# A fifth landing tile for weight pieces, a later split of the probabilities, and two overlapped output quarters in a two-layer decoder trunk

## The chip, the cores and the metric

The kernel runs on one core of one Trainium2 chip. The metric is the device time of one execution in microseconds (us). The kernel before took 2178.07 us, the median of three runs (2176.98 to 2179.72).

## What is computed

The reference runs two decoder layers on 256 tokens of width 2048, all in float32. Layer 0 mixes with a gated spatial unit and a linear recurrence (mixer A and B), layer 1 with 16 heads of attention that has a forget gate (mixer C). Each mixer is followed by a gated MLP with a short convolution.

```python
for l in range(DEPTH):                       # DEPTH = 2
    h = rms_norm(x, mix_norm[l])
    if l % 2 == 0:
        h = mixer_ab(h, ab_w_in[j], ...)     # 2048 -> 6144 columns, then w_out 2048 x 2048
    else:
        h = mixer_c(h, c_w_in[j], ...)       # 2048 -> 4 * 2048 + 16 columns, then w_out
    x = x + h
    h = rms_norm(x, ffn_norm[l])
    x = x + conv_ffn(h, ffn_w_up[l], ...)    # 2048 -> 2 * 5632, conv of width 3, 5632 -> 2048

# mixer C, for each block of 128 queries and each head:
s = q @ k.T * scale + c[query] - c[key]      # c: running sum of the log of the forget gate
p = softmax(where(causal, s, -inf))
o = p @ v
return (concat(o) * sigmoid(g)) @ w_out
```

## The kernel before, in words

**Weights.** Every weight is read once, in pieces of 128 x 1024 numbers (512 KB). A piece is good for 12 matmuls of 512 columns: two rows of 128 inputs (k and k + 1), two halves T of the tokens, and three products each, because every float32 operand is split in a high part and a rest that together carry the precision (high x high, high x low, low x high). One piece is called a step here. `weights` makes a piece: `three` takes a landing tile `w` and two tiles `wh` and `wl`, SyncE (SP) issues the load of `w`, ScalarE (ACT) copies `w` to `wh` (L178), VectorE (DVE) subtracts to get `wl` (L179), and TensorE (PE) then reads `wh` and `wl`. The tile `w` comes free when its `wl` is made. The main pool has four tiles `w` and three of `wh` and `wl` (`wpool, pool, nw, ns = wp, wp, 4, 3`). In the MLPs two of every five pieces, after the twelfth, use tiles of a second pool, and in mixer C every fourth piece has its `wh` and `wl` in one.

**Order.** Loads of `w`, copies to `wh` and subtractions to `wl` each keep the order of the pieces. Everything else is a Python generator that `tick` moves on by one `yield` a step, so that a `yield` is a delay by one piece. `held` keeps an instruction behind the newest `wh` or `wl`. What a queue holds next to the pieces, and where, follows from that and from the order in which the framework lays the instructions out; the engines then run their queues in order.

**Turning.** Matmuls give tokens on partitions; many steps need features there. `blocks` turns 32 x 32 blocks on DVE, `moves` then sends 16 small transfers of 32 KB (L360), eight on SP's queue and eight on GpSimd's (POOL), from `tmp` to a tile that is named `turn`, `dst`, `o` or `zt`.

**Attention (mixer C).** Four groups of four heads; for each group three projections of eight steps (q, k, v), by `project_tok`. `turn_rows` normalises and turns q and k. `attend` works on two heads: it copies and splits their q and k (`k`, `kk`, `qq`, L1012 to L1016), multiplies them, takes the softmax, turns the probabilities by 16 transfers from POOL (`pt`, L1058), waits `LAG + 2` = 8 yields, splits `pt` in `ph` (ACT, L1067) and `pl` (DVE, L1068), and multiplies with v; ACT copies the result to `o` (L1082). After the groups come four steps-of-eight projections for the gate (`w_cg`); `gate` multiplies the gate, turned, with `o` (DVE, L1160) and splits the products into `yc` (ACT L392, DVE L394), four of them for each quarter.

**Output of attention.** `w_co` is multiplied in four quarters q of 512 output columns, each over all 16 `yc` (k = 0, 2, ... 14), by `project_four`; `product(k)` gives `yc` number k. Then `add_four` turns the result and adds it to `x`. The output of mixer A and B, in layer 0, has another order: the last two pieces of its quarter 0 come after four pieces of quarter 1 (the function `stretch` of that mixer).

**Small tiles.** The constants `cst` hold four blocks of 128 columns, the last of them, K_REV, a reversed identity. `ra` and `rb` serve one reversal of row scales in `mirror`; `rs` is a tile of 64 columns for each of the four groups, of which eight columns are used.

Of the kernel before, what the change touches and what calls it, by code (L numbers as in the profile page):

```python
# [8 lines left out]
F32 = mybir.dt.float32  # L9
F32R = mybir.dt.float32r  # L10
U16 = mybir.dt.uint16
AF = mybir.ActivationFunctionType
ALU = mybir.AluOpType
AX = mybir.AxisListType

P = 128
S = 256
D = 2048
KT = D // P
NH = 8  # L20
CH = 16
# [3 lines left out]
BLK = 32  # L25
LAG = 6
# [7 lines left out]
LANE = 64  # L34
# [11 lines left out]
K_ID, K_TRI, K_CM, K_REV = 0, 128, 256, 384  # L46
NK = K_REV + P
# [7 lines left out]
def tile_trunk(ctx: ExitStack, tc: tile.TileContext, x, pp_d, cst_d, mlev_d, msk_d,  # L55
               w_v, w_f, w_g, w_i, w_q, w_u, w_abo, w_cf, w_cqkv, w_cg, w_co, w_up, w_dn, spw_d, spb_d, out):
    nc = tc.nc
    V, SC, PE = nc.vector, nc.scalar, nc.tensor

    cp = ctx.enter_context(tc.tile_pool(name="cp", bufs=1))  # L60
    wp = ctx.enter_context(tc.tile_pool(name="wp", bufs=4))
    apool = ctx.enter_context(tc.tile_pool(name="ap", bufs=KT))
    tp = ctx.enter_context(tc.tile_pool(name="tp", bufs=2))
# [4 lines left out]
    def nm(base):  # L68
        count[0] += 1
        return f"{base}_{count[0]}"  # L70

    xT = []
    xload = []
    for c0, n in ((0, 1), (1, 1), (2, 2), (4, 2), (6, 2), (8, 4), (12, 4)):
        t = cp.tile([P, n, S], F32, tag=f"x{c0}", name=f"x{c0}")
# [1 line left out]
        xT += [t[:, i] for i in range(n)]  # L77
    part = {c0 + i: (t, i, c0 + n - 1) for t, c0, n in xload for i in range(n)}
    pp = cp.tile([P, -(-NPP // LANE) * LANE], F32, tag="pp", name="pp")
    cst = cp.tile([P, NK], F32, tag="cst", name="cst")  # L80
    ones = cp.tile([P, P], F32, tag="ones", name="ones")
    one1 = cp.tile([P, LANE], F32, tag="one1", name="one1")[:, 0:1]

# [40 lines left out]
    flight, queue = [], []  # L124
# [38 lines left out]

    def three(n):
        deep["turn"] += 1
        wpool, pool, nw, ns = wp, wp, 4, 3
        if deep["pool"] is not None:
            if deep["more"] == 2 and deep["turn"] > 12 and deep["turn"] % 5 in (1, 3):
                wpool, pool, nw, ns = deep["pool"], deep["pool"], 2, 2
            elif deep["more"] == 1 and deep["turn"] % 4 == 3:  # L170
                pool, ns = deep["pool"], 1
        w = wpool.tile([P, n], F32, tag="w", name=nm("w"), bufs=nw)
        wh = pool.tile([P, n], F32R, tag="wh", name=nm("wh"), bufs=ns)
        wl = pool.tile([P, n], F32R, tag="wl", name=nm("wl"), bufs=ns)
        return w, wh, wl
# [150 lines left out]
    def project_four(w4, acts, n, k0=0, ks=None, ps=None, more=False):  # L326

        begun = ps is not None
        ps = ps or [pm.tile([P, 512], F32, tag="pm", name=nm("pm")) for _ in range(2)]
        ks = ks or range(0, n, 2)  # L330
        for k in ks:
            tick()
            lo = (k0 + k) * P
            wh, wl = weights(w4[:, :, lo:lo + 2 * P].rearrange("m p c -> p m c"), 1024, 4)
            for T in range(2):
                for i in range(2):
                    a = acts(k + i) if callable(acts) else acts[k + i]
                    ah, al = a[:, T * P:(T + 1) * P], a[:, S + T * P:S + (T + 1) * P]
                    h, l = (by_rows(t, i) for t in (wh, wl))
                    PE.matmul(to_rows(ps[T]), ah, h, start=not begun and k + i == ks[0], stop=False)  # L340
                    PE.matmul(to_rows(ps[T]), ah, l, start=False, stop=False)  # L341
                    deep["mm"] = deep["last"] = PE.matmul(to_rows(ps[T]), al, h, start=False,  # L342
                                                          stop=not more and k + i == ks[-1] + 1)
        return ps
# [39 lines left out]
    def held(r, last="wh"):  # L384

        tc.add_manual_dep(r.ins, deep[last].ins.name, order, reason="not before")
# [69 lines left out]
            rsq(Rt, p2[:, 0:4].rearrange("p (t two) -> p t two", two=2)[:, :, 0], D)  # L456
            self.Rt = Rt

    def add_x(m, ps):
        t = tp.tile([P, S], F32, tag="ev", name=nm("ev"), bufs=3)  # L460
        SC.activation(t, ps[:, S:2 * S], AF.Copy)
        V.tensor_tensor(xT[m], xT[m], ps[:, 0:S], ALU.add)
        V.tensor_tensor(xT[m], xT[m], t, ALU.add)

    def add_four(q, ps, z, tmp, dst, nxt, halves=1, queues=(nc.sync, nc.gpsimd)):
        for T in range(2):
            SC.activation(cols4(z[:, T]), of_rows(ps[T]), AF.Copy)
# [23 lines left out]
    def mixer_ab(norm):  # L491
        es = ExitStack()
        hp = es.enter_context(tc.tile_pool(name="hp", bufs=1))
# [19 lines left out]
        for g, ps in enumerate(project_first(w_v, norm, lambda: queue.append(finish()))):  # L513
            v = hp.tile([P, 2, 512], F32, tag="tok", name=nm("gv"), bufs=2)
# [10 lines left out]
        def fetch_late(*args, behind="wh"):  # L525
            r = SC.dma_start(*args)
            tc.add_manual_dep(r.ins, deep[behind].ins.name, order, reason="queue order")

        fetch_late(cst, cst_d, behind="hold")
        fetch_late(pp[:, C_FFN:C_CW], pp_d[:, C_FFN:C_CW], behind="hold")  # L530
        def wide(n):
            return hp.tile([P, 1024], F32, tag="QK", name=nm(n), bufs=2)
# [77 lines left out]


        Rr = hp.tile([P, LANE], F32, tag="Rr", name="Rr")[:, 0:2]
        ra, rb = (hp.tile([P, LANE], F32, tag=n, name=n)[:, 0:BLK] for n in ("ra", "rb"))

        def mirror():
            yield
            held(V.tensor_copy(ra, Rt[:, 1:2].to_broadcast([P, BLK])), "wl")
            V.tensor_copy(Rr[:, 0:1], Rt[:, 0:1])
            V.transpose(rb, ra)
            V.transpose(ra, view(rb, BLK - 1, (-1, BLK)))  # L620
            for a in range(4):
                V.tensor_copy(Rr[BLK * (3 - a):BLK * (4 - a), 1:2], ra[BLK * a:BLK * (a + 1), 0:1])
# [41 lines left out]
        for j in range(2):  # L664
            ps = project_four(w_f[4 * j:4 * j + 4], A, KT)
# [3 lines left out]
            t = hp.tile([P, 1024], F32, tag="o", name=nm("turn"), bufs=2)  # L669
# [5 lines left out]
        itoks, left, os_ = [], [NH], []  # L675
# [154 lines left out]
        for h in range(NH):  # L830
# [6 lines left out]
            ps = project(w_q[h], A)  # L837
            for T in range(2):
                q = kq[h][:, 2 - T]
                SC.activation(back(q) if T else q, view(ps, T, (2, P)), AF.Copy, scale=omlb[:, h:h + 1])  # L840
            queue.append(hgrn(h))
        for j in range(2):
            ps = project_four(w_g[4 * j:4 * j + 4], A, KT)
# [16 lines left out]
        for j in range(2):  # L860
            ps = project_four(w_u[4 * j:4 * j + 4], A, KT)
# [3 lines left out]
            t = hp.tile([P, 1024], F32, tag="tok", name=nm("turn"), bufs=2)  # L865
# [15 lines left out]
        ahead = None  # L881
        for q in range(4):
            if q == 0:

                ps = stretch(0, (0, 2, 4, 6, 8, 10), more=True)
                ahead = stretch(1, (0, 2, 4, 6), more=True)
                stretch(0, (12, 14), ps=ps)
            elif q == 1:
                ps = stretch(1, (8, 10, 12, 14), ps=ahead)
            else:  # L890
                ps = stretch(q, range(0, KT, 2))
# [11 lines left out]
    def mixer_c(norm):  # L903
        es = ExitStack()
        hp = es.enter_context(tc.tile_pool(name="cpool", bufs=1))
# [86 lines left out]
            V.tensor_copy(ct, ps[:, 0:S].rearrange("p (t c) -> p t c", t=2)[..., 0:CH])  # L992

        left, soft = [CH], [CH]
        os_, rss = [], []

        turn = [0]

        def attend(hs, q, k, v, o, rs, mark):

            while len(mark) < 2 or steps[0] < max(turn[0], mark[1] + LAG + 2):
                yield
# [45 lines left out]
            for i, sms in enumerate(sums):  # L1048
                t = V.transpose(tmp.rearrange("p (b m i) -> p b m i", b=4, m=6)[:, :, 3 * i:3 * i + 3],
                                sc[:, 3 * i:3 * i + 3].rearrange("p m (b j) -> p b m j", b=4))  # L1050
# [3 lines left out]
            n = 6 * BLK  # L1054
            pt = hp.tile([P, 6, P], F32, tag="pt", name=nm("pt"), bufs=2)
            for a in range(4):
# [3 lines left out]
                                        .rearrange("p (m r) -> p m r", m=6))  # L1060
                if a == 1:
                    yield
            for _ in range(LAG + 2):
                yield
            pair = [hp.tile([P, 2, S], F32R, tag=n, name=nm(n), bufs=1) for n in ("ph", "pl")]
            near = pt.rearrange("p (i m) q -> p i (m q)", i=2)[:, :, 0:S]
# [43 lines left out]
        for g in range(CH // 4):  # L1110
            qkv, mark = [], []
            ss = hp.tile([P, 2, 2, LANE // 4], F32, tag="ss", name=nm("ss"), bufs=2)[..., 0:4]
            for j in range(3):
                if g == 0 and j == 2:
                    cd = []
                    queue.append(sums(*forget()))
                if g and j == 2:
                    spread(g)
                ps = early[j] if g == 0 and j < 2 else project_tok(w_cqkv[j * (CH // 4) + g], norm)
                if j == 2:  # L1120
                    vs = [hp.tile([P, 512], F32R, tag=n, name=nm(n), bufs=2) for n in ("vh", "vl")]
                    v1 = hp.tile([P, 512], F32, tag="v", name=nm("v"), bufs=2)
                    SC.activation(cols2(vs[0]), of_two(ps[0]), AF.Copy, scale=Rt[:, 0:1])
                    SC.activation(cols2(v1), of_two(ps[1]), AF.Copy, scale=Rt[:, 1:2])
                    V.scalar_tensor_tensor(cols2(vs[1]), of_two(ps[0]), Rt[:, 0:1], cols2(vs[0]).bitcast(F32),
                                           ALU.mult, ALU.subtract)
                    qkv.append((vs, v1))
                    break
                t = piece("turn", 4)
                start(turn_rows(ps, ss, j, heads(t), mark))  # L1130
                qkv.append(heads(t))
            if g == 0:
                columns(cd[1])
            os_.append(heads(piece("o", CH // 4)))
            rss.append(hp.tile([P, LANE], F32, tag="rs", name=nm("rs"), bufs=CH // 4)[:, 0:8]
                       .rearrange("p (t h) -> p t h", t=2))
            queue.extend(attend((h, h + 1), *qkv, os_[g], rss[g], mark) for h in range(4 * g, 4 * g + 4, 2))

        room, places = [], [("big", 4, 1)] + 2 * [("vh", 1, 2), ("vl", 1, 2)] + 4 * [("o", 2, CH // 4)]
        depth[0] = 3  # L1140
# [30 lines left out]
        for q in range(CH // 4):  # L1171
            ps = project_four(w_cg[4 * q:4 * q + 4], A, KT)
# [4 lines left out]
        def product(k):  # L1177
            while yB[k] is None:
                tick()
            return yB[k]  # L1180

        nxt = Norm(C_FFN + KT, turn=True)
        depth[0] = 2
        for q in range(4):
            ps = project_four(w_co[4 * q:4 * q + 4], product, KT)
            add_four(q, ps, piece("z", 2), flat(piece("tmp", 2)), heads(piece("turn", 4)), nxt)
        deep["pool"] = None
        es.close()
# [232 lines left out]
```

## Time and profile before

| | |
|---|---|
| median of 3 runs | 2178.07 us |
| the profiled execution | 2179.36 us |
| its span | 2177.6 us |
| PE busy | 2167.3 us (100%) |
| DVE busy | 1599.6 us (73%) |
| ACT busy | 1313.4 us (60%) |
| POOL busy | 472.0 us (22%) |
| granted clock of PE | 1.00 in every stage |

The profiled execution's time lies 1.8 us above its span, and 1.3 us above the median. Busy time of PE counts each matmul from its start to a modelled end, 0.38 us for 512 columns, though the next one starts after 0.216 us; so a hole of PE shows in the profile as idle time only beyond about 0.16 us, and is read better from the starts of the matmuls. Layer 0's mixer lies at 0 to 392 us of the span, its MLP at 392 to 1063 us, mixer C at 1063 to 1515 us, and its MLP after that.

### The profile page before, as it was taken

How to read it: one execution, taken by the hardware profiler on the slowest of the kernel's cores; microseconds unless marked ns; L12 is line 12 of the kernel's file. 1: busy time of each engine (PE TensorE's matmuls, PEld its weight loads, DVE VectorE, ACT ScalarE, POOL GpSimd, SP SyncE). 2: the span in 40 equal slices, each digit the busy share in tenths (PEclk: the TensorE clock that was granted, in tenths of full speed). 3: DMA queues.
4: the chain of work that ended last, by engine and by line, in shares of the span. 5: the costliest groups of instructions: out<-in, count | busy, mean ns of one | idle time of the engine just before them, and what ended most of it. 6: DMA issues, size and time to landing. Idle time of an engine off the chain costs nothing.

```text
span 2177.6 us, 32602 instructions
## 1 busy us (share of the span) xinstructions
PE 2167.3 (100%) x10874; PEld 1900.8 (87%) x10874; DVE 1599.6 (73%) x2286; ACT 1313.4 (60%) x1951; POOL 472.0 (22%) x865
## 2 busy tenths in 40 slices
PE   9999999999999999999999999999999999999999
PEld 8988888888888888888888888888888888888888
DVE  7788768777567757776987786877776577667766
ACT  7678766666556545654565566766666466456642
POOL 0252222212012002111133444212211012011202
PEclk9999999999999999999999999999999999999999
DMA  8655687877676766776777767777777677766866
GB/s 300 205 164 175 200 243 225 249 229 236 210 226 209 237 210 210 229 241 206 234 227 229 219 216 215 223 238 235 231 227 240 196 230 219 228 213 204 255 211 189
DMA packets 492617, 483.62 MB, mean 222 GB/s; under 512 B 115136, under 2 KB 460240, under 8 KB 492320
## 3 DMA queue, kind: packets, MB, share of 16 engines
q1 hardware_dynamic: 465888, 453.27, 66.6%
q0 software_dynamic: 24832, 25.92, 5.1%
q10 hardware_dynamic: 1728, 2.35, 0.3%
q8 instruction: 85, 1.39, 0.3%
q14 instruction: 84, 0.69, 0.1%
HBM read 435.24 MB, written 2.11 MB: 201 GB/s over the span
## 4 chain that ended last, share of the span: by engine, by line
PE 90%; DVE 3%; DMA 2%; ACT 2%; issue 1%; SPq 1%; POOL 0%; ACTq 0%; DVEq 0%; POOLq 0%
PE pm L341 25%; PE pm L342 25%; PE pm L340 25%; PE pm L322 3%; PE pm L321 3%; PE pm L323 3%; PE pm L297 1%; DVE wl L179 1%; PE pm L229 1%; SPq L360 1%; ACT wh L178 1%; PE pm L253 1%; DMA pt<-ptmp 1%; DMA w<-in_w_f 0%; DVE kq L734 0%
## 5 line engine op out<-in xcount | busy, mean ns | idle before, releaser
L179 DVE TENSOR_TENSOR wl<-w,wh 128x1024 fp32r<-128x1024 f32 (+1 forms) x820 | 990.5, 1218 | 452.4 <-ACT wh L178 440.5
L178 ACT ACTIVATE wh<-w 128x1024 fp32r<-128x1024 f32 (+1 forms) x820 | 855.4, 1049 | 611.7 <-PE pm L342 437.4
L341 PE MATMUL pm<-wl,a 128*128 128x512 f32 x1728 | 655.6, 379 | 0.9 <-DVE wl L179 0.8
L340 PE MATMUL pm<-wh,a 128*128 128x512 f32 x1728 | 655.9, 380 | 0.0
L342 PE MATMUL pm<-wh,a 128*128 128x512 f32 x1728 | 654.9, 379 | 0.0
L360 POOL DMA_DIRECT2D zt<-tmp x413 | 224.3, 551 | 1133.8 <-DVE tmp L353 1021.7
L341 PEld LDWEIGHTS pm<-wl,a 128*128 128x128 f32 x1728 | 326.6, 189 | 49.0 <-DVE wl L179 3.1
L340 PEld LDWEIGHTS pm<-wh,a 128*128 128x128 f32 x1728 | 326.5, 189 | 46.2
L342 PEld LDWEIGHTS pm<-wh,a 128*128 128x128 f32 x1728 | 326.6, 189 | 46.1
L340 PE MATMUL pm<-wh,hid 128*128 128x512 f32 x688 | 260.8, 379 | 0.0
L341 PE MATMUL pm<-wl,hid 128*128 128x512 f32 x688 | 260.8, 379 | 0.0
L342 PE MATMUL pm<-wh,hid 128*128 128x512 f32 x688 | 260.8, 379 | 0.0
L322 PE MATMUL pm<-wl,a 128*128 128x512 f32 x416 | 158.2, 380 | 2.5 <-DVE wl L179 2.4
L321 PE MATMUL pm<-wh,a 128*128 128x512 f32 x416 | 158.6, 381 | 0.0
L323 PE MATMUL pm<-wh,a 128*128 128x512 f32 x416 | 157.8, 379 | 0.0
L342 PEld LDWEIGHTS pm<-wh,hid 128*128 128x128 f32 x688 | 130.0, 189 | 18.5
L340 PEld LDWEIGHTS pm<-wh,hid 128*128 128x128 f32 x688 | 130.0, 189 | 18.5
L341 PEld LDWEIGHTS pm<-wl,hid 128*128 128x128 f32 x688 | 130.0, 189 | 18.4
L360 POOL DMA_DIRECT2D turn<-tmp x160 | 87.2, 553 | 244.0 <-DVE tmp L353 156.1
L1227 ACT ACTIVATE conv<-zt,pp 128x256 f32<-128x256 f32 x176 | 95.8, 589 | 65.8 <-DMA zt<-tmp 54.0
L1228 DVE SCALAR_TENSOR_TENSOR conv<-zt,pp,conv 128x255 f32<-128x255 f32 x176 | 80.1, 480 | 49.6 <-ACT conv L1227 33.4
L353 DVE STREAM_TRANSPOSE tmp<-z 128x512 f32<-128x512 f32 x120 | 98.3, 856 | 7.2 <-ACT z L1213 5.1
(252 smaller groups left out, 2246.3 us busy)
## 6 DMA issues: line engine op xcount, KB each, us to landing
w<-in_w_up SPq DMA_DIRECT2D x352, 512.0 KB, 4.9
w<-in_w_dn SPq DMA_DIRECT2D x176, 512.0 KB, 4.9
w<-in_w_cqkv SPq DMA_DIRECT2D x96, 512.0 KB, 4.7
w<-in_w_abo SPq DMA_DIRECT2D x32, 512.0 KB, 4.8
w<-in_w_cg SPq DMA_DIRECT2D x32, 512.0 KB, 4.6
w<-in_w_co SPq DMA_DIRECT2D x32, 512.0 KB, 4.7
zt<-tmp SPq DMA_DIRECT2D x414, 32.0 KB, 2.6
zt<-tmp POOLq DMA_DIRECT2D x413, 32.0 KB, 2.5
```

Of the source, the lines that this page charges most:

```text
L178: r = deep["wh"] = SC.activation(wh, w, AF.Copy)
L179: deep["wl"] = V.tensor_tensor(wl, w, wh.bitcast(F32), ALU.subtract)
L321: PE.matmul(to_two(ps[T]), ah, h, start=k + i == 0, stop=False)
L322: PE.matmul(to_two(ps[T]), ah, l, start=False, stop=False)
L323: deep["last"] = PE.matmul(to_two(ps[T]), al, h, start=False, stop=k + i == KT - 1)
L340: PE.matmul(to_rows(ps[T]), ah, h, start=not begun and k + i == ks[0], stop=False)
L341: PE.matmul(to_rows(ps[T]), ah, l, start=False, stop=False)
L342: deep["mm"] = deep["last"] = PE.matmul(to_rows(ps[T]), al, h, start=False, stop=not more and k + i == ks[-1] + 1)
L353: V.transpose(tmp.rearrange("p (b m i t) -> p b m i t", b=4, m=4, t=2)[:, :, :, :, T], src(T).rearrange("p (m b j) -> p b m j", m=4, b=4))
L360: queues[(a + b) % len(queues)].dma_start(dst[BLK * b:BLK * (b + 1), :, a * n:(a + 1) * n], tmp[BLK * a:BLK * (a + 1), b * 4 * n:(b + 1) * ...
L1227: held(SC.activation(c, z, AF.Identity, bias=pp[:, cb:cb + 1], scale=w(2)))
L1228: V.scalar_tensor_tensor(c[:, 1:], z[:, :S - 1], w(1), c[:, 1:], ALU.mult, ALU.add)
```

## The change

Three edits and some that make room for them.

1. The main pool's landing tiles `w` go from four to five. The room comes from `cst`, which loses the block K_REV (nothing reads it), from `ra` and `rb`, which become two parts of a tile `junk` that exists already, and from the four tiles `rs`, which become parts of one.
2. `attend` waits `LAG + more` yields before it splits the probabilities: 11 in place of 8 for the first three groups, 8 as before for the last.
3. The last two pieces (k = 12 and 14) of quarter 0 of attention's output come after the first two pieces (k = 0 and 2) of quarter 1. Four accumulators are then open at once.

A function `add_x` that nothing called goes as well.

```diff
-    cst = cp.tile([P, NK], F32, tag="cst", name="cst")
+    cst = cp.tile([P, K_REV], F32, tag="cst", name="cst")
...
-        wpool, pool, nw, ns = wp, wp, 4, 3
+        wpool, pool, nw, ns = wp, wp, 5, 3
...
-        fetch_late(cst, cst_d, behind="hold")
+        fetch_late(cst, cst_d[:, 0:K_REV], behind="hold")
...
-        ra, rb = (hp.tile([P, LANE], F32, tag=n, name=n)[:, 0:BLK] for n in ("ra", "rb"))
...
+            r = hp.tile([P, 512], F32, tag="junk", name=nm("junk"), bufs=1)
+            ra, rb = (r[:, i * BLK:(i + 1) * BLK] for i in range(2))
...
+        rsum = hp.tile([P, LANE], F32, tag="rs", name="rs")
...
-        def attend(hs, q, k, v, o, rs, mark):
+        def attend(hs, q, k, v, o, rs, mark, more):
...
-            for _ in range(LAG + 2):
+            for _ in range(LAG + more):
                 yield
...
-            queue.extend(attend((h, h + 1), *qkv, os_[g], rss[g], mark) for h in range(4 * g, 4 * g + 4, 2))
+            rss.append(rsum[:, 8 * g:8 * g + 8].rearrange("p (t h) -> p t h", t=2))
+            queue.extend(attend((h, h + 1), *qkv, os_[g], rss[g], mark, 5 if g < CH // 4 - 1 else 2) for h in range(4 * g, 4 * g + 4, 2))
...
+        def stretch(q, ks, **kw):
+            return project_four(w_co[4 * q:4 * q + 4], product, KT, ks=ks, **kw)
+
         nxt = Norm(C_FFN + KT, turn=True)
         depth[0] = 2
+        ahead = None
         for q in range(4):
-            ps = project_four(w_co[4 * q:4 * q + 4], product, KT)
+            if q == 0:
+                ps = stretch(0, range(0, 12, 2), more=True)
+                ahead = stretch(1, (0, 2), more=True)
+                stretch(0, (12, 14), ps=ps)
+            elif q == 1:
+                ps = stretch(1, range(4, KT, 2), ps=ahead)
+            else:
+                ps = stretch(q, range(0, KT, 2))
```

**SP's queue at the end of the last group of attention.** The rows are the loads of pieces for v (`in_w_cqkv`) and for the gate (`in_w_cg`), and the eight transfers that turn the last group's k. Before:

```order
L191 DMA w_12953<-in_w_cqkv 128x1024
L191 DMA w_12971<-in_w_cqkv 128x1024
L191 DMA w_12989<-in_w_cqkv 128x1024
L191 DMA w_13017<-in_w_cg 128x4x256
L360 DMA turn_12795<-tmp_12797 32x4x64 x8
L191 DMA w_13035<-in_w_cg 128x4x256
L191 DMA w_13069<-in_w_cg 128x4x256
```

And after:

```order
L191 DMA w_12952<-in_w_cqkv 128x1024
L191 DMA w_12974<-in_w_cqkv 128x1024
L191 DMA w_13013<-in_w_cg 128x4x256
L191 DMA w_13031<-in_w_cg 128x4x256
L360 DMA turn_12788<-tmp_12790 32x4x64 x8
L191 DMA w_13065<-in_w_cg 128x4x256
L191 DMA w_13110<-in_w_cg 128x4x256
```

One more load stands ahead of the turning transfers: two pieces of the gate in place of one.

**ACT's queue at the same place.** The rows are copies of pieces (`wh`), of the next two heads' k and q (`k`, `kk`, `qq`), the copies of v's accumulators (`vh`, `v`), and, after, the results of a pair of heads of the group before (`o`). Before:

```order
L1012 ACTIVATE k_2302_13061<-turn_12795,gq 128x128
L1013 ACTIVATE kk_13062<-turn_12795,gq 128x256
L1014 ACTIVATE qq_13063<-turn_12561 128x128
L178 ACTIVATE wh_13070<-w_13069 128x1024
L1123 ACTIVATE vh_13007<-pm_12801,Rt_10562 128x512
L1124 ACTIVATE v_13009<-pm_12802,Rt_10562 128x512
L178 ACTIVATE wh_13115<-w_13114 128x1024
L178 ACTIVATE wh_13133<-w_13132 128x1024
```

And after:

```order
L1008 ACTIVATE k_2299_13057<-turn_12788,gq 128x128
L1009 ACTIVATE kk_13058<-turn_12788,gq 128x256
L1010 ACTIVATE qq_13059<-turn_12558 128x128
L178 ACTIVATE wh_13066<-w_13065 128x1024
L1119 ACTIVATE vh_12992<-pm_12794,Rt_10561 128x512
L1120 ACTIVATE v_12994<-pm_12795,Rt_10561 128x512
L178 ACTIVATE wh_13111<-w_13110 128x1024
L1078 ACTIVATE o_12319<-px_13001 128x2x128
L1078 ACTIVATE o_12319<-px_13002 128x2x128
L178 ACTIVATE wh_13129<-w_13128 128x1024
```

The two copies to `o`, which stood three copies of pieces earlier, now follow the copies of v. The same is found at the ends of the two groups before.

**ACT's queue where the last quarter's products are made.** The rows are copies of `w_co` pieces (`wh`) and the four splits to `yc` number 12 to 15. Before, the four `wh` ahead of the first `yc` are those of quarter 0 with k = 8, 10, 12 and 14, and the next is quarter 1's first:

```order
L178 ACTIVATE wh_13996<-w_13995 128x1024
L178 ACTIVATE wh_14016<-w_14015 128x1024
L178 ACTIVATE wh_14037<-w_14036 128x1024
L178 ACTIVATE wh_14057<-w_14056 128x1024
L392 ACTIVATE yc_13992<-turn_13894 128x256 x2
L178 ACTIVATE wh_14100<-w_14099 128x1024
L392 ACTIVATE yc_14033<-turn_13894 128x256 x2
```

After, they are quarter 0's k = 8 and 10 and quarter 1's k = 0 and 2, and the next two are quarter 0's k = 12 and 14:

```order
L178 ACTIVATE wh_13992<-w_13991 128x1024
L178 ACTIVATE wh_14012<-w_14011 128x1024
L178 ACTIVATE wh_14035<-w_14034 128x1024
L178 ACTIVATE wh_14055<-w_14054 128x1024
L392 ACTIVATE yc_13988<-turn_13890 128x256
L178 ACTIVATE wh_14073<-w_14072 128x1024
L392 ACTIVATE yc_13988<-turn_13890 128x256
L392 ACTIVATE yc_14031<-turn_13890 128x256 x2
L178 ACTIVATE wh_14091<-w_14090 128x1024
```

The splits keep their place among the copies; what moved is which pieces lie ahead of them.

More of the change, by code (lines that the diff above doesn't have):

```diff
@@ L457, in finish_tok @@
             self.Rt = Rt
[L459 to L463, printed above, removed]
     def add_four(q, ps, z, tmp, dst, nxt, halves=1, queues=(nc.sync, nc.gpsimd)):
@@ L1134, in mixer_c @@
             os_.append(heads(piece("o", CH // 4)))
-            rss.append(hp.tile([P, LANE], F32, tag="rs", name=nm("rs"), bufs=CH // 4)[:, 0:8]
-                       .rearrange("p (t h) -> p t h", t=2))
-            queue.extend(attend((h, h + 1), *qkv, os_[g], rss[g], mark) for h in range(4 * g, 4 * g + 4, 2))
+            rss.append(rsum[:, 8 * g:8 * g + 8].rearrange("p (t h) -> p t h", t=2))
+            queue.extend(attend((h, h + 1), *qkv, os_[g], rss[g], mark, 5 if g < CH // 4 - 1 else 2) for h in range(4 * g, 4 * g + 4, 2))
         room, places = [], [("big", 4, 1)] + 2 * [("vh", 1, 2), ("vl", 1, 2)] + 4 * [("o", 2, CH // 4)]
```

## The prediction

> **What bounds the kernel now.** I read the page first, then the busy time by stage, the table of waits with PE's rows alone, and then the timeline around each wait of PE. The page:
>
> ```profile
> span 2177.6 us, 32602 instructions
> PE 2167.3 (100%) x10874; PEld 1900.8 (87%) x10874; DVE 1599.6 (73%) x2286; ACT 1313.4 (60%) x1951; POOL 472.0 (22%) x865
> ```
>
> PE is the bound. The stages (length, then PE's busy time and its matmuls in brackets, then the other engines) show where it has holes; the last column is what the DMA engines moved in GB/s:
>
> ```profile
> 100.00:192.00 92.00, 89.31 (x936) 81.40 (x938) 74.80 (x142) 71.31 (x199) 46.69 (x84) 1.00 0.58 174
> ...
> 392.00:1063.00 671.00, 671.00 (x3111) 587.39 (x3109) 480.47 (x644) 389.48 (x518) 112.98 (x208) 1.00 0.73 222
> ...
> 1515.00:2155.00 640.00, 640.00 (x2967) 560.41 (x2966) 451.30 (x592) 369.65 (x480) 104.41 (x193) 1.00 0.73 223
> ```
>
> In the two MLPs PE has no hole at all: 671.00 us for 3111 matmuls is 0.216 us from start to start, which no edit here changes, since the same matmuls run. So only a hole outside the MLPs can be gained. PE's waits are few:
>
> ```profile
> PE pm L322 <- DVE wl L179: 2.4, 3, 1.0
> PE pm L341 <- DVE wl L179: 1.3, 3, 0.5
> ...
> PE pm L340 <- ACT yc L392: 0.7, 1, 0.7
> ```
>
> A matmul's modelled end lies 0.16 us behind the next start, so each hole is larger than its entry. I size each by PE's starts: the time between two starts less 0.216 us for every matmul between them.
>
> **Edit 3, the overlapped quarters.** The three kinds of rows below are PE's, DVE's and ACT's timelines at the end of quarter 0 of attention's output.
>
> ```profile
> 1419.09 0.38 PE L342 MATMUL pm<-wh,yc 128*128 128x512 f32 x1
> 1420.17 0.48 PE L340 MATMUL pm<-wh,yc 128*128 128x512 f32 x1 [0.71 <-ACT yc L392]
> ...
> 1424.34 0.38 PE L340 MATMUL pm<-wh,yc 128*128 128x512 f32 x1
> ```
>
> ```profile
> 1419.00 1.43 DVE L1160 TENSOR_TENSOR turn<-turn,o 128x256 f32<-128x256 f32 x4 [2.36 <-DMA turn<-tmp]
> ```
>
> ```profile
> 1419.45 1.32 ACT L392 ACTIVATE yc<-turn 128x256 fp32r<-128x256 f32 x2 [4.08 <-DVE turn L1160]
> ```
>
> PE needs `yc` number 12 right after its row at 1419.09. The split starts at 1419.45, since the last turning transfer ended DVE's wait only at 1419.00. The row at 1424.34 is sixteen matmuls behind that at 1419.09: 5.25 - 16 x 0.216 = 1.79 us are lost. After the change 24 matmuls of quarter 1 stand there first, 24 x 0.216 = 5.2 us, for which `yc` 0 to 3 have long been made. Their pieces have their `wh` ahead of the first split in ACT's queue, as the order shows. `yc` number 12 is then wanted at 1424.5 and is there by 1421; its own piece's `wh` follows the first split (1420.1 to 1421.1), its `wl` the first rest on DVE (to about 1422.3). The last three splits, at 0.66 us, end by 1423.2. So the cover is longer than what is late, and the hole goes whole: -1.79 us. Nothing is late next: quarter 0's accumulators are copied out while quarter 1 runs six pieces more, and quarters 2 and 3 keep their places. If the cover failed, at worst what it costs now comes back.
>
> **Edit 1, the fifth landing tile.** PE waits three times in mixer C for a `wl`:
>
> ```profile
> 1253.43 0.38 PE L321 MATMUL pm<-wh,a 128*128 128x512 f32 x1
> ...
> 1254.18 0.38 PE L323 MATMUL pm<-wh,a 128*128 128x512 f32 x1
> ```
>
> ```profile
> 1318.00 0.38 PE L340 MATMUL pm<-wh,a 128*128 128x512 f32 x1
> ...
> 1318.61 0.38 PE L342 MATMUL pm<-wh,a 128*128 128x512 f32 x1
> ...
> 1320.77 0.38 PE L340 MATMUL pm<-wh,a 128*128 128x512 f32 x1
> ...
> 1321.82 0.38 PE L342 MATMUL pm<-wh,a 128*128 128x512 f32 x1
> ```
>
> Each pair is two matmuls apart: 0.75, 0.61 and 1.05 us less 0.43 each, together 1.12 us. What made the `wl` late is seen on ACT and SP:
>
> ```profile
> 1240.57 0.86 ACT L1082 ACTIVATE o<-px 128x256 f32<-128x256 f32 x2
> 1248.24 1.06 ACT L178 ACTIVATE wh<-w 128x1024 fp32r<-128x1024 f32 x1 [6.80 <-PE pm L322]
> ...
> 1253.60 1.04 ACT L178 ACTIVATE wh<-w 128x1024 fp32r<-128x1024 f32 x1
> ```
>
> ```profile
> 1239.06 5.11 SPq L360 DMA_DIRECT2D turn<-tmp  x8
> 1244.27 9.90 SPq L191 DMA_DIRECT2D w<-in_w_cqkv  x6
> ```
>
> ```profile
> 1315.91 1.06 ACT L178 ACTIVATE wh<-w 128x1024 fp32r<-128x1024 f32 x1 [7.33 <-DMA w<-in_w_cg]
> ```
>
> SP spends 5.1 us on issuing eight turning transfers while landing tiles come free; the next load goes out at 1244.27 and ACT can copy it at 1248.24, after 6.8 us of idleness (put down to PE, but PE's wait had long ended; the second place, 1315.91, names the load). PE then lives on pieces made before, and these run out 5 us later. In the changed order one more load stands ahead of the turning transfers. A piece is 12 x 0.216 = 2.6 us of PE's time, more than any of the three holes, so all go: -1.12 us.
>
> The same happens once in the first mixer's output:
>
> ```profile
> 296.74 0.38 PE L340 MATMUL pm<-wh,yb 128*128 128x512 f32 x1
> ...
> 297.91 0.38 PE L342 MATMUL pm<-wh,yb 128*128 128x512 f32 x1
> ```
>
> ```profile
> 292.73 0.54 ACT L99 ACTIVATE zu<-turn 128x256 f32<-128x256 f32 x1 [2.50 <-DMA turn<-tmp]
> ...
> 295.23 1.06 ACT L178 ACTIVATE wh<-w 128x1024 fp32r<-128x1024 f32 x1 [0.90 <-DMA w<-in_w_abo]
> ```
>
> 1.17 - 0.43 = 0.74 us are lost, and the `wh` waited for its load. With a load more in hand it can follow the copy that ends at 293.3, nearly two microseconds sooner: -0.74 us.
>
> The holes of the stage 100 to 192 us, the largest sum (2.7 us idle), are another matter:
>
> ```profile
> 129.39 1.04 ACT L178 ACTIVATE wh<-w 128x1024 fp32r<-128x1024 f32 x1
> ```
>
> ```profile
> 132.90 1.22 DVE L179 TENSOR_TENSOR wl<-w,wh 128x1024 fp32r<-128x1024 f32 x1
> ```
>
> ```profile
> 134.18 0.48 PE L322 MATMUL pm<-wl,a 128*128 128x512 f32 x1 [1.03 <-DVE wl L179]
> ```
>
> Here `wh` is done at 130.4 and DVE comes to the `wl` only at 132.90, behind the recurrence's work in its queue. The load was long there; a fifth tile can't help, and I take nothing (bounds: 0 and -2.7 us). In the MLPs the tile has no hole to fill: nothing.
>
> [...]
>
> ```profile
> w<-in_w_cqkv SPq DMA_DIRECT2D x96, 512.0 KB, 4.7
> ...
> turn<-tmp SPq DMA_DIRECT2D x160, 32.0 KB, 2.2
> turn<-tmp POOLq DMA_DIRECT2D x160, 32.0 KB, 2.2
> ```
>
> Turning transfers land after 2.2 us from SP's queue, where loads stand ahead, and after 2.2 us from POOL's, where none do: no price is seen for standing behind loads, and I take none. [...]
>
> **Edit 2, the later split.** It moves, for six of eight pairs of heads, one copy on ACT, one subtraction on DVE, eight short matmuls and two copies to `o` by three pieces; no DMA moves, since POOL has issued `pt` before the delay. The split waited at times:
>
> ```profile
> 1232.89 0.63 ACT L1067 ACTIVATE ph<-pt 128x512 fp32r<-128x512 f32 x1 [3.92 <-DMA pt<-ptmp]
> ```
>
> With the three pieces, 7.8 us, that wait goes; but PE had no hole within 20 us of it, so it is worth nothing by itself. What the edit costs is ACT's load where the `o` copies land, between the copies of v and the next `wh`. From 1248.24 to 1254.64 ACT works without a pause, 6.4 us for three pieces; with 0.86 us for `o` it is 7.3 us, still under the 7.8 us that PE takes for three. Cost 0; bounds 0 and 0.86 + 0.63 us at each of three group ends.
>
> The smaller `cst`, the shared `junk` and `rs` change no wait of PE: 0.
>
> **The sum.** -1.79 - 1.12 - 0.74 = -3.65 us. The profiled execution took 2179.36 us, 1.29 above the median of 2178.07; it would take 2175.7, and the median becomes 2174.4 us. That is 0.17% faster. About 0.2%, or 4.4 us, is what a measurement of this kernel can tell from no change, since three runs spread over 2.7 us.
>
> **The rivals.**
>
> *More than that.* Holes of the first mixer shift too, because the load order there moves by one piece. Against it: no `wh` waits for a load between 100 and 192 us. For it: a changed order may by chance fit better. All 2.7 us: 2171.7 us. Chance 0.15.
>
> *The fifth tile does nothing for PE.* The pieces are late because ACT and DVE run in order, not for want of a tile. For it stands DVE's row at 132.90; against it, the loads named at 1315.91 and 295.23. Then only edit 3 counts: 2178.07 - 1.79 = 2176.3 us. Chance 0.14.
>
> [...] Chance 0.05. [...]
>
> *Slower: ACT at the group ends.* If the copies to `o` and the split, 1.49 us, do not fit beside the next heads' k and q and v, a wait of that size at each of three group ends replaces those that were there: 3 x 1.49 = 4.5, the 1.12 is not gained, 1.79 and 0.74 are: +1.9, or 2180.0 us. It decides once ACT needs over 7.8 us in three pieces and has used up the piece of lead that the fifth tile gives, 2.6 us. For it: two of the three holes in mixer C lie right at this place. Against: 7.3 is under 7.8. Chance 0.11.
>
> **The numbers.** The forecast has the remaining 0.55, and its own range is 2173 to 2176. The range of 2171.5 to 2179.5 leaves out a tenth above (the slower rival) and some 6% below. Faster by over 0.2% (below 2173.7): the first rival and a third of the forecast's range, 0.32. Slower by over 0.2% (above 2182.4): the last rival at twice its price, 0.06. Within: 0.62.
>
> **What would show it.** After: PE has no wait for `yc`; no hole of PE at the group ends of mixer C; ACT's idle 6.8 and 7.3 us there are shorter by about one piece; the hole near 297 us is gone; those between 100 and 192 us stay, 2.7 us; the MLPs keep 0.216 us a matmul. A new hole behind `o` at a group end, or any in the MLPs, makes the prediction wrong.

## The result and the profile after

The changed kernel takes 2175.63 us, the median of 20 runs (2174.37 to 2177.20), against 2179.11 us for the kernel before on the same chip (20 runs, 2176.23 to 2182.12). The ratio is 0.9985 [0.9978, 0.9991]. That is 3.48 us less, where 3.65 were forecast: a change of under 0.2%, with an interval that leaves out no change at all. So sign and size came out as predicted; the experiments show that not every step of the sum did.

The page of the changed kernel; its profiled execution took 2175.11 us, with a span 4.3 us shorter:

```profile
span 2173.3 us, 32509 instructions
PE 2164.5 (100%) x10874; PEld 1900.8 (87%) x10874; DVE 1602.1 (74%) x2286; ACT 1315.8 (61%) x1951; POOL 471.4 (22%) x865
```

Busy time by stage, with the columns of before: length, PE, weight loads, DVE, ACT, POOL, granted clock, DMA share, GB/s.

```profile
100.00:192.00 92.00, 88.63 (x947) 80.57 (x946) 74.56 (x144) 70.41 (x195) 46.78 (x83) 1.00 0.55 173
392.00:1063.00 671.00, 671.00 (x3110) 587.17 (x3109) 480.32 (x646) 389.38 (x518) 112.69 (x208) 1.00 0.72 222
...
1515.00:2155.00 640.00, 640.00 (x2967) 560.44 (x2966) 452.69 (x591) 368.10 (x475) 107.66 (x199) 1.00 0.71 222
```

The MLPs are as they were, and 100 to 192 us keeps its holes: 3.4 us idle against 2.7. The table of waits, with PE's rows alone:

```profile
PE pm L322 <- DVE wl L179: 3.0, 3, 1.7
PE warm L145 <- DVE ones L85: 1.1, 1, 1.1
PE pm L341 <- DVE wl L179: 0.4, 1, 0.4
PE pm L297 <- DVE wl L179: 0.3, 1, 0.3
```

No row names `yc` any more. PE's timeline where quarters 0 and 1 of attention's output meet:

```profile
1415.21 0.38 PE L342 MATMUL pm<-wh,yc 128*128 128x512 f32 x1
...
1425.14 0.38 PE L340 MATMUL pm<-wh,yc 128*128 128x512 f32 x1
```

The second row is 46 matmuls behind the first: 9.93 us, or 46 x 0.216. The hole of 1.79 us is gone. ACT's timeline at the first mixer's output:

```profile
293.87 1.06 ACT L178 ACTIVATE wh<-w 128x1024 fp32r<-128x1024 f32 x1 [0.57 <-PE pm L342]
...
296.46 1.06 ACT L178 ACTIVATE wh<-w 128x1024 fp32r<-128x1024 f32 x1 [0.66 <-PE pm L342]
```

And at the first group end that the prediction spoke of:

```profile
1246.39 1.05 ACT L178 ACTIVATE wh<-w 128x1024 fp32r<-128x1024 f32 x1
1247.34 0.84 ACT L1078 ACTIVATE o<-px 128x256 f32<-128x256 f32 x2
1249.56 1.06 ACT L178 ACTIVATE wh<-w 128x1024 fp32r<-128x1024 f32 x1 [1.38 <-PE pm L323]
```

The copies to `wh` now wait for PE to give a tile back (0.57, 0.66 and 1.38 us), not for a load. PE's holes at these places are gone. ACT's idle stretches of 6.8 and 7.3 us at the two group ends are gone as well: the longest there is now 1.5 us, so they shrank by two pieces, where about one was forecast. One hole stands at 1370 us, where the first profile of before has none, and it comes about in the last group, whose split kept its 8 yields. ACT, DVE and PE there, in this order:

```profile
1359.47 0.82 ACT L1078 ACTIVATE o<-px 128x256 f32<-128x256 f32 x2
...
1366.46 0.63 ACT L1063 ACTIVATE ph<-pt 128x512 fp32r<-128x512 f32 x1 [5.72 <-DMA pt<-ptmp]
```

```profile
1368.47 1.17 DVE L179 TENSOR_TENSOR wl<-w,wh 128x1024 fp32r<-128x1024 f32 x1
```

```profile
1368.91 0.38 PE L340 MATMUL pm<-wh,a 128*128 128x512 f32 x1
1369.70 0.48 PE L341 MATMUL pm<-wl,a 128*128 128x512 f32 x1 [0.41 <-DVE wl L179]
```

ACT stands 5.7 us in front of `ph`, since `pt` is still on its way; what lies behind it is late, and PE loses 0.79 - 0.22 = 0.57 us. The prediction had no such wait. It is the trace of what follows.

### The profile page after: what moved, and what is told of

Read it like the earlier page. It is cut to its first block, busy times and chain, and to the rows that moved or that the text cites. A ratio compares the mean times of both kernels' runs of the same rounds, so it can differ in the third digit from the quotient of the medians.

```text
span 2173.3 us, 32509 instructions
## 1 busy us (share of the span) xinstructions
PE 2164.5 (100%) x10874; PEld 1900.8 (87%) x10874; DVE 1602.1 (74%) x2286; ACT 1315.8 (61%) x1951; POOL 471.4 (22%) x865
## 4 chain that ended last, share of the span: by engine, by line
PE 94%; DVE 2%; ACT 1%; DMA 1%; issue 1%; POOL 0%; SPq 0%; ACTq 0%; DVEq 0%
PE pm L340 26%; PE pm L341 26%; PE pm L342 26%; PE pm L322 4%; PE pm L321 4%; PE pm L323 4%; PE pm L229 1%; PE pm L297 1%; DVE wl L179 1%; DMA pt<-ptmp 1%; ACT wh L178 1%; PE pm L253 1%; DVE kq L729 0%; DVE st L758 0%; ACT E L725 0%
```

## The experiments

Each kernel was timed against the kernel before on the same chip; differences are read from the ratios, since the medians of before range from 2179.1 to 2180.8 us over the chips. The difference of the two medians can lie up to 1 us away from that. At the end a table gives PE's holes in every profile.

### The edits one by one

**Edit 3 alone,** on the kernel before:

```diff
-            ps = project_four(w_co[4 * q:4 * q + 4], product, KT)
+            if q == 0:
+                ps = stretch(0, range(0, 12, 2), more=True)
+                ahead = stretch(1, (0, 2), more=True)
+                stretch(0, (12, 14), ps=ps)
+            elif q == 1:
+                ps = stretch(1, range(4, KT, 2), ps=ahead)
...
```

> The kernel before with the two overlapped output quarters alone. Theory (each hole has its own cause): the 1.79 us at the end of quarter 0 go, PE has no wait for yc; the three holes at attention's group ends (1.12 us) and the one near 297 us (0.74) stay. About -1.8 us against the kernel before. Rival (the fifth tile is what frees the last quarter, since its loads come sooner): a hole before the yc matmuls remains, under 1 us gained.

Measured: 2178.08 against 2180.34 us, ratio 0.9994 [0.9985, 1.0002], or -1.3 us with an interval from -3.3 to +0.4. The hole for `yc` is gone from the profile, as it is in all the profiles with overlapped quarters. But the holes at the group ends and at 297 us are absent too, but for 0.2 us, with four tiles, where edit 1 was to be what removes them.

**Edit 1 alone,** five tiles and the room that they need:

```diff
-        wpool, pool, nw, ns = wp, wp, 4, 3
+        wpool, pool, nw, ns = wp, wp, 5, 3
```

> The changed kernel with four output quarters one after the other and the split after 8 yields for all groups: what is left is the fifth landing tile and the room made for it. Theory: the holes at the group ends (1.12 us) and near 297 us (0.74) go, the 1.79 us for yc stay; about -1.9 us. Rival (the later split is what removed the holes at the group ends): 1.12 us stay there, about -0.7 us. Also open: whether the holes near 70, 381 us and at the end, which the changed kernel lost as well (1.5 us), go with the tile or come and go by chance.

Measured: 2185.70 us, ratio 1.0027 [1.0017, 1.0038]. The tile, with the room made for it, costs 0.27%, 5.9 us (5.4 by the medians), where -1.86 us was its term in the sum. The room alone was not run with the early split; it is part of the next kernel, which loses nothing. PE's waits in this kernel:

```profile
PE pm L322 <- DVE wl L179: 8.6, 6, 2.6
PE pm L341 <- DVE wl L179: 0.8, 2, 0.5
PE pm L342 <- DVE yc L394: 0.6, 2, 0.5
PE pm L340 <- ACT yc L392: 0.6, 2, 0.3
```

Three new holes of 2.75, 1.75 and 1.72 us stand near 1173, 1242 and 1310 us, one in each of the first three groups.

**Edit 2 alone,** with four tiles and quarters in sequence (the smaller `cst`, `junk` and `rs` stay as in the changed kernel):

```diff
-            for _ in range(LAG + 2):
+            for _ in range(LAG + more):
...
+            queue.extend(attend(..., mark, 5 if g < CH // 4 - 1 else 2) ...)
```

> The changed kernel with four landing tiles and four output quarters one after the other: the later split alone. Theory: it moves no hole of PE, 0 us; the holes at the group ends (1.12 us) stay. Rival (ACT's wait for the turned probabilities is what made the pieces late there): they go, -1.1 us.

Measured: 2180.84 us, ratio 1.0004 [0.9995, 1.0013]. With four tiles the later split is worth nothing, as forecast.

**The changed kernel without edit 2:**

```diff
-            queue.extend(attend(..., mark, 5 if g < CH // 4 - 1 else 2) ...)
+            queue.extend(attend(..., mark, 2) ...)
```

> The changed kernel with the split after 8 yields for all groups. Theory: within 0.5 us of the changed kernel, -3.5 us against before; the group ends stay free of holes, and the new hole of 0.7 us near 1370 us is still there, since it belongs to the last group, whose split was not moved. Rival: the later split does part of the work, and 1.1 us of holes come back.

Measured: 2184.56 us, ratio 1.0017 [1.0008, 1.0026]. The changed kernel has 0.9985 and, in a second measurement below, 0.9979: with five tiles the later split is worth 0.32 to 0.38%, 7 to 8 us. Behind it stand 6.2 us of holes (the `pt` column of the table below) and, in a part of the runs, PE's clock, as the last section shows. The two edits depend on each other. The mechanism can be read in this kernel's trace, first ACT, then DVE, then PE, at the end of the first of the holes:

```profile
1158.91 1.05 ACT L178 ACTIVATE wh<-w 128x1024 fp32r<-128x1024 f32 x1
1159.86 0.84 ACT L1078 ACTIVATE o<-px 128x256 f32<-128x256 f32 x2
1167.13 0.63 ACT L1063 ACTIVATE ph<-pt 128x512 fp32r<-128x512 f32 x1 [6.43 <-DMA pt<-ptmp]
...
1168.01 3.88 ACT L178 ACTIVATE wh<-w 128x1024 fp32r<-128x1024 f32 x4
```

```profile
1167.79 0.69 DVE L1064 TENSOR_TENSOR pl<-pt,ph 128x512 fp32r<-128x512 f32 x1 [5.69 <-ACT ph L1063]
...
1170.21 1.30 DVE L353 STREAM_TRANSPOSE tmp<-z 128x512 f32<-128x512 f32 x2
1171.43 4.59 DVE L179 TENSOR_TENSOR wl<-w,wh 128x1024 fp32r<-128x1024 f32 x4
```

```profile
1169.64 0.38 PE L321 MATMUL pm<-wh,a 128*128 128x512 f32 x1
1172.67 0.48 PE L322 MATMUL pm<-wl,a 128*128 128x512 f32 x1 [2.65 <-DVE wl L179]
```

ACT reaches `ph` at 1160.7 and stands there for 6.43 us. Behind it in its queue lie four `wh`, of which the first starts only at 1168.01, and the normalisation of k; DVE stands in front of `pl` for 5.69 us, then has the normalisation and the turning to do, and comes to the next `wl` only at 1171.43. PE has used its pieces by then. In the kernel before, the same place reads, on ACT and then on DVE:

```profile
1162.01 1.06 ACT L178 ACTIVATE wh<-w 128x1024 fp32r<-128x1024 f32 x1 [1.41 <-DMA w<-in_w_cqkv]
...
1165.53 0.63 ACT L1067 ACTIVATE ph<-pt 128x512 fp32r<-128x512 f32 x1 [1.73 <-DMA pt<-ptmp]
```

```profile
1166.20 0.69 DVE L1068 TENSOR_TENSOR pl<-pt,ph 128x512 fp32r<-128x512 f32 x1 [1.28 <-ACT ph L1067]
...
1167.14 1.23 DVE L179 TENSOR_TENSOR wl<-w,wh 128x1024 fp32r<-128x1024 f32 x1 [0.17 <-ACT wh L178]
...
1168.88 1.29 DVE L1105 TENSOR_TENSOR z<-z,ss 128x512 f32<-128x512 f32 x2
```

There ACT was held up by loads on its way, and so came to `ph` when `pt` was nearly there: at 1163.80, 3.1 us later than with five tiles, while `pt` itself was there 1.6 us sooner. The order of the queues differs too: before, one `wl` stands between `pl` and the normalisation and is made at 1167.14; with five tiles none does, so that the wait and the normalisation hold up the same four pieces one after the other. The table of waits has this for the whole kernel. ACT's waits for loads in attention and for `pt`, before:

```profile
ACT wh L178 <- DMA w<-in_w_cqkv: 22.9, 14, 6.2
...
ACT ph L1067 <- DMA pt<-ptmp: 8.4, 3, 3.9
```

With five tiles and the early split:

```profile
ACT ph L1063 <- DMA pt<-ptmp: 22.1, 4, 6.4
ACT wh L178 <- DMA w<-in_w_cqkv: 9.0, 5, 3.7
```

With five tiles and the later split, the changed kernel:

```profile
ACT ph L1063 <- DMA pt<-ptmp: 5.7, 1, 5.7
...
ACT wh L178 <- DMA w<-in_w_cqkv: 0.9, 2, 0.7
```

The fifth tile took waits for loads away and gave them to `pt`, whose transfers take about as long as they did (by the median 4.8 us from issue to landing before and in the changed kernel, 4.9 with five tiles and the early split). Edit 2 takes most of that second wait away.

### How steady the holes are

**Edits 2 and 3 without the tile:** the changed kernel with `wp, wp, 4, 3`.

> The changed kernel with four landing tiles in place of five: the later split and the overlapped quarters stay. Theory as it stands after the first four runs (the fifth tile saves load waits at the group ends, near 297 us and at 70 us, and the later split pays for the wait that it brings): 1 to 2 us slower than the changed kernel, about -2 us against before. Rival (the holes that I gave to the fifth tile come and go by chance, and the tile is worth nothing): within 0.5 us of the changed kernel, -3.5 us against before.

Measured: 2178.91 against 2180.76 us, ratio 0.9993 [0.9984, 1.0001]. **The later split in the last group too,** with `mark, 5)` for all:

> The changed kernel with the split after 11 yields for the last group too. Theory: the hole of 0.7 us near 1370 us goes, since ACT's wait of 5.7 us for the turned probabilities there ends before the split; the last group's results come 7.8 us later, and the first gate quarters' products have room for that: about 0.7 us faster than the changed kernel, -4.2 us against before. Rival: the products of the gate come too late and a hole of up to 2 us opens before the output projection at 1400 us.

Measured: 2175.64 us, ratio 0.9978 [0.9969, 0.9987]. The hole at 1370 us is gone, and the time is that of the changed kernel. **The changed kernel again:**

> The changed kernel, unchanged, for a second profile and for the time on the same chip as the others. Theory: -3.5 us against before; the hole near 1370 us is there again, since a wait in program order makes it; holes between 100 and 192 us sum to some 4 us again; the places near 70, 297 and 381 us have none. What differs from the first profile is chance.

Measured: 2176.16 us, ratio 0.9979 [0.9970, 0.9988]; the hole at 1370 us is there again. So, given the later split, the fifth tile is worth some 2.7 us (2178.91 less 2176.16, on one chip). The two intervals against before overlap a little, but the fastest run with four tiles, 2177.63 us, is slower than the slowest with five, 2177.05. **The kernel before again,** one execution:

> The kernel before, unchanged, for a second profile. Theory (the holes that I gave to the fifth tile have a cause in the program): three holes at the group ends (1.1 us) and one near 297 us (0.7), as in the first profile. Rival (they depend on how the loads fall in an execution): at least two of the four are not there, as in the profiles of the overlap alone and of the split alone.

Measured: 2178.67 us. The hole at 297 us, 0.74 us in the first profile, isn't there, and those at the group ends sum to 0.7 us in place of 1.1, the small ones counted in. The hole for `yc` is there again, and larger. A small one of 0.28 us stands at 1370.8 us, so that place isn't quite free of holes before either. So the places that I had given to the tile change from one execution to the next. In the kernel with four tiles and edits 2 and 3, ACT waits for a load elsewhere, near 46 us, where the first profile of before had no hole:

```profile
44.85 1.06 ACT L178 ACTIVATE wh<-w 128x1024 fp32r<-128x1024 f32 x1 [1.53 <-PE pm L229]
51.20 1.06 ACT L178 ACTIVATE wh<-w 128x1024 fp32r<-128x1024 f32 x1 [5.30 <-DMA w<-in_w_f]
```

PE loses 0.98 and 0.91 us at 54 and 60 us there. Holes of over 0.25 us between 54 and 61 us are found in three of the five profiles with four tiles, and in none of the nine with five.

### Two ways to test the wait for `pt`

**One piece later in place of three,** 9 yields in the first three groups:

```diff
-            queue.extend(attend(..., mark, 5 if g < CH // 4 - 1 else 2) ...)
+            queue.extend(attend(..., mark, 3 if g < CH // 4 - 1 else 2) ...)
```

> The changed kernel with the split after 9 yields for the first three groups, one piece (2.6 us) later than the kernel without the later split, two pieces sooner than the changed one. Theory (with five tiles ACT no longer waits for loads, reaches the split of the second pair early and stands there until the turned probabilities land, 6.4 us, with copies of pieces behind it): the wait shrinks by about 2.6 to 3.8 us, and the holes of 2.8, 1.7 and 1.7 us near 1173, 1243 and 1312 us shrink to under 0.5 us together; time within 1.5 us of the changed kernel. Rival (the holes come from the order of the pieces' subtractions behind the normalisation on DVE, not from the wait): they stay, 4 us slower than before.

**The early split on an engine that has time,** POOL, with five tiles and 8 yields everywhere:

```diff
-            held(SC.activation(pair[0], near, AF.Copy))
-            held(V.tensor_tensor(pair[1], near, pair[0].bitcast(F32), ALU.subtract), "wl")
+            nc.gpsimd.tensor_copy(pair[0], near)
+            nc.gpsimd.tensor_tensor(pair[1], near, pair[0].bitcast(F32), ALU.subtract)
```

> The changed kernel with the split after 8 yields everywhere, and with both halves of it, the copy and the subtraction, on GpSimd in place of ACT and DVE. Theory: the wait for the turned probabilities then stands in GpSimd's queue, where no piece is behind it; the holes near 1173, 1243, 1312 and the one near 1370 us go, though five tiles and 8 yields are kept; time near the changed kernel's, -3 to -4.5 us against before. Rival (loads crowd the DMA engines, so the pieces themselves come late): the holes stay, 4 us slower than before. What could spoil it: the next turning transfers from GpSimd start behind the split, some 5 us later, and q and k of the next group with them.

Measured on one chip: 9 yields 2176.71 us, ratio 0.9983 [0.9974, 0.9992]; POOL 2176.61 us, 0.9982 [0.9973, 0.9991]. Both have the time of the changed kernel. With 9 yields ACT still waits 15.6 us for `pt`, but of the three holes one of 0.53 us is left: a piece is 2.6 us, and the longest hole was 2.8. With the split on POOL the wait is all there, on another engine:

```profile
POOL ph L1063 <- DMA pt<-ptmp: 30.1, 7, 6.4
...
ACT wh L178 <- DMA w<-in_w_cqkv: 7.9, 5, 2.1
```

POOL stands 30.1 us in front of `pt`, up to 6.4 us at a time, as ACT did with five tiles and the early split (22.1 us, up to 6.4), and the three holes are gone. The one at 1370 us is gone too, but two of 0.55 and 0.53 us stand at 1384 and 1393 us, which were not followed. What cost PE its time is thus shown to be the place of the wait, in ACT's and DVE's queues ahead of `wh` and `wl`, and not the transfer. Of the two kernels, this one separates the wait from the normalisation: DVE still does that ahead of four `wl`, from 1163.49 us, and no hole follows. With 9 yields one more `wl` also stands ahead of `pl`, so that kernel alone could not tell the two apart; but it leaves ACT and DVE the work of the split, which rules out that the work itself made the holes.

### The holes that stayed

The largest sum of holes, between 118 and 202 us, belongs to the first mixer's recurrence, whose heads start `PACE` = 4 pieces apart. Two kernels change that in the changed kernel:

```diff
-PACE = 4
+PACE = 5
```

> The changed kernel with the heads of the first mixer's recurrence started five pieces apart in place of four. Theory (the holes of some 4 us near 134, 137, 164 and 186 us stand because DVE's and ACT's queues hold the recurrence's work ahead of the pieces): with that work spread over more pieces they shrink, by 1 to 3 us, unless the recurrence then ends too late for its output projection, which would show as waits for yb. Rival (they come from something else in that stretch, such as GpSimd's copies for the i projection): they stay, within 0.5 us of the changed kernel.

> The same with six pieces. Theory: the holes near 134 to 186 us shrink further than with five, but the last head starts 14 pieces (36 us) later than in the changed kernel, and the output projection at 280 us may wait for it. Rival as for five pieces: the holes stay.

Measured on one chip: PACE = 5 2178.04 against 2180.45 us, ratio 0.9991 [0.9982, 1.0000]; PACE = 6 2190.09 us, 1.0045 [1.0032, 1.0057]. With 5 the holes there shrink from 4.0 to 2.2 us, but 1.9 us of new ones come between 202 and 292 us and 1.0 at 1064. With 6 PE has none of them, but 3.4 us of others between 202 and 292 us, and it stands once for a result that the recurrence hands over too late:

```profile
PE pm L340 <- ACT yb L392: 10.2, 1, 10.2
```

No version beat the changed kernel by more than its interval.

### The holes in one table

Each number sums, over a stretch of the span, by how much matmuls started later than their forerunner's columns allow (0.216 us for 512, from 671.00 us for 3110 matmuls in the MLP), where that was over 0.25 us. In us, by the profile of each kernel:

| kernel | 50-76 | 118-202 | 292-306 | 1140-1246 and 1275-1314 (`pt`) | 1246-1275 and 1314-1335 (group ends) | 1335-1398 | 1398-1440 (`yc`) |
|---|---|---|---|---|---|---|---|
| before | 0.65 | 3.59 | 0.64 | 0 | 0.52 | 0 | 1.28 |
| before, again | 0.68 | 3.93 | 0 | 0 | 0.48 | 0.28 | 1.99 |
| edit 3 alone | 1.67 | 3.91 | 0 | 0 | 0 | 0 | 0 |
| edit 2 alone | 1.67 | 3.14 | 0 | 0 | 0 | 0 | 0.97 |
| edits 2 and 3 | 2.79 | 4.11 | 0 | 0 | 0 | 0 | 0 |
| edit 1 alone | 0.66 | 4.09 | 0 | 6.22 | 0 | 0.49 | 1.93 |
| edits 1 and 3 | 0.52 | 3.78 | 0 | 6.24 | 0 | 0.57 | 0 |
| changed kernel | 0 | 4.03 | 0 | 0 | 0 | 0.57 | 0 |
| changed kernel, again | 0.34 | 3.96 | 0 | 0 | 0 | 0.54 | 0 |
| 9 yields | 0.58 | 4.24 | 0 | 0.53 | 0 | 0.76 | 0 |
| split on POOL | 0 | 3.67 | 0 | 0 | 0 | 1.07 | 0 |

## Why the prediction was right, and where it was not

**Edit 3, -1.79 us: right.** The hole is there in both profiles of before and in both kernels with quarters in sequence, and in none with the overlap. In full it was 1.8 to 2.3 us in before and 1.3 us with edit 2 alone, so the term's size is right to about half a microsecond. The time of edit 3 alone agrees (-1.3 us), with an interval too wide to prove it by itself.

**Edit 1, -1.12 and -0.74 us: the sum was met by luck.** The cause named at the group ends holds, its size doesn't, and a cost is left out. The holes named are gone in the changed kernel. But they are nearly gone, too, in three kernels with four tiles, and the one at 297 us was absent when the kernel before was profiled again. Their sizes were those of one execution. At the two group ends the wait for a load is real and comes back, and the hole is what of it goes beyond some 6.5 us: in the two profiles of before and with edit 3 alone, ACT's waits of 7.33, 7.17 and 6.74 us go with holes of 0.80, 0.59 and 0.19 us at the second group end, and waits of 6.80, 6.62 and 5.82 us with 0.32, 0.10 and none at the first. So a few tenths of a microsecond of a load decide the size. What five tiles do in every profile is to shorten ACT's waits for the loads of q, k and v (22.9 and 36.0 us in the two profiles of before, 0.9 and 2.1 in those of the changed kernel). With the later split that is worth some 2.7 us, part of which shows near 50 to 76 us, a place that the prediction did not name. Without it, it costs 5.9 us.

**Edit 2, 0: this is the step that failed.** It was put as "PE had no hole within 20 us of it, so it is worth nothing by itself", with bounds of 0 and a loss. By itself that is what edit 2 alone shows. The mistake was to price it in the order of before, while edit 1 changes when ACT arrives at `ph`. In the changed kernel the same edit is worth 7 to 8 us: it pays for the wait that the fifth tile makes. The two errors, a harmful tile counted as a gain and a needed delay counted as nothing, cancel, because the change holds both edits: a sum that fits is no sign here that its terms do. Had the prediction been for the tile alone, its sign would have been wrong.

**What would show it.** By the text a new hole behind `o` at a group end makes the prediction wrong. The one at 1370 us comes close: it lies behind `o` on ACT, in the gate's pieces after the last group. Its cause is `ph`, not the copies to `o` after v that the slower rival spoke of, and it costs nothing that can be measured (0.9978 with the later split in all groups, 0.9979 without). At the group ends proper no hole is seen, so ACT's 7.3 us did fit there.

**The rivals.** More than forecast: the holes of the first mixer stayed, 4.0 us against 3.6 to 3.9. The tile does nothing: this gave -1.79 us, just outside the changed kernel's interval of -4.8 to -2.0, and the kernels above refute it in both directions. The turning transfers land no later for the load more that stands ahead of them: at the last group's end the eight on SP's queue take 2.1 us by the median, and took 2.2 before, and over the whole kernel, where both medians were 2.2 us before, they are now:

```profile
turn<-tmp SPq DMA_DIRECT2D x160, 32.0 KB, 2.2
turn<-tmp POOLq DMA_DIRECT2D x160, 32.0 KB, 2.1
```

**What stays open.** The span fell by 4.3 us and the holes over 0.25 us by only 2.7; the rest is spread over many small ones, which were not followed. Why holes near 50 to 60 us come with four tiles in some executions and not in others was not settled either: a load that is late at 46 us is seen, its reason is not.

## What to carry to other kernels

Here, with the early split, a deeper buffer didn't only remove a wait: as ACT's waits for loads fell from 22.9 to 9.0 us, ACT arrived earlier at the next thing that it must wait for, `pt`; its waits there rose from 8.4 to 22.1 us, and what lay behind that in its queue stood with it. So price two edits together when one changes the arrival of the other, and look for the next wait in the queue of the engine that is freed. A hole of less than a microsecond in one profile, like that of 0.74 us which a second one didn't have, is not yet a term of a sum; profile the unchanged kernel twice first.

## What was not expected of the hardware

In one profile a hole of 2.81 us was followed by a lower clock. After the 2.65 us wait at 1172.67 in the kernel with edits 1 and 3, PE's rows read:

```profile
1173.70 0.63 PE L322 MATMUL pm<-wl,a 128*128 128x512 f32 x1
1174.13 0.63 PE L323 MATMUL pm<-wh,a 128*128 128x512 f32 x1
```

They are 0.43 us apart in place of 0.216, as are the row ahead of them and the next five; the stretch has a granted clock of 0.81:

```profile
1170.00:1175.00 5.00, 2.35 (x8) 1.86 (x8) 5.00 (x7) 1.89 (x2) 3.20 (x6) 0.81 0.25 48
```

The hole cost 2.81 us by PE's starts, and the slow matmuls behind it some 1.7 more. The same stretch with edit 1 alone, whose hole is 2.75 us, has a clock of 1.00:

```profile
1170.00:1175.00 5.00, 2.41 (x12) 1.85 (x11) 5.00 (x6) 2.13 (x3) 2.95 (x6) 1.00 0.22 42
```

In that execution, whose granted clock is 1.000, its holes of 1.75 and 1.72 us were not followed by a lower one either. With `PACE` = 6, PE's rows behind the wait of 10.15 us are 0.43 us apart too, up to 301.69 us, and the stretch from 270 to 310 us has a clock of 0.87. How often it happens can be seen in the granted clock of each run. With edits 1 and 3 it is 1.000 in five of eleven runs, which took 2181.45 to 2182.98 us, and 0.998 or 0.999 in the other six, which took 2184.56 to 2186.05; with edit 1 alone four of seven are below 1.000; of the changed kernel's 31 runs none is. So with edits 1 and 3 some 3 us of the price come and go with the clock; with edit 1 alone the clock doesn't sort the times. Why only one of two like holes was followed by a lower clock was not shown.
